# Layer 1's mixer: sixteen weight tiles split one stage ahead, the solve's copies and merges spread among products, the convolution's branch within the scan

## The chip, the cores and the metric

The kernel runs on one core of a Trainium2 chip. The metric is device time in microseconds (us) from one launch, on inputs that lie in HBM. Five engines work side by side on their own instruction queues: PE (TensorE, matmuls; PEld are its weight loads), DVE (VectorE), ACT (ScalarE), POOL (GpSimd) and SP (SyncE, which here issues nearly all DMA transfers). Each takes its instructions strictly in the order written at build time, and waits at one until what it needs is there.

## The reference

A backbone of two layers over 512 tokens: 256 context tokens and 256 latent tokens, 1024 channels, in fp32. Context tokens read only context; the latent scans start from the context's final state.

```python
for l in range(2):
    h += 0.5 * gate1 * swiglu(mod(rmsnorm(h)), ffn1)          # "ffn1"
    n = mod(rmsnorm(h)); p = n @ w_in                         # "mixer"
    a = conformer_conv(p[conv])          # GLU, 31 taps per row of 64, LayerNorm, silu, @ conv_proj
    q, k, v = silu(short_conv(p[qkv]))   # 3 taps; q, k normalised
    o = gated_delta_rule(q, k, v, ...)   # 8 heads, two directions, in chunks: a triangular solve, then a scan
    b = (rmsnorm(o) * onorm * silu(p[z])) @ dn_proj
    h += gate2 * ((sigmoid(p[ga]) * a + sigmoid(p[gb]) * b) @ w_out)
    h += 0.5 * gate3 * swiglu(mod(rmsnorm(h)), ffn2)          # "ffn2"
out = rmsnorm(h_latent)
```

## The kernel before

**Products.** Activations lie with channels on the 128 partitions and tokens in columns. An fp32 product is made of three passes on tiles rounded to a short format: high by high, high by low, low by high. So every weight tile of 128 x 8 x 128 values (512 KB) passes three steps in `weights`: SP loads it into `raw` (L124; the pool `rawp` has 3 buffers), ACT writes its rounded half `whi` (L117), DVE writes the rest `wlo` as `raw` minus `whi` (L118; the pool `wp` has 3 buffers for each half). Then PE makes 24 matmuls from it into a bank of PSUM named `pm` (L147). The bank is emptied by ACT or DVE, and there are 4 of them. Other uses of PSUM share 4 banks named `px`. In layer 1 the gates, the convolution and q need only the latent tokens (256 columns, in the rows `128x256`); k and v need all 512.

**Background.** `beside` hands a stage a list of jobs, and every call of `weights` draws from it at an even rate. In ffn1 of layer 0 there are 57 jobs for 64 calls (the modulation's `ada` weights: a load of 512 KB and four DVE instructions each); in ffn1 of layer 1 there are 24 for 64.

**The mixer**, in the order of its code:

- the convolution's input (GLU), k and q, with their norms;
- `todo`, a list of 32 products: 8 gate tiles each of z, ga and gb (`gate`: ACT empties the bank into `gz` at L964 and stores it to DRAM), then 8 value tiles (`value`: a short convolution on ACT and DVE, L450 and L451, then transposes by PE, L976). `some(n)` writes out the next n of them;
- `gram` and `solve`: the triangular blocks of 32 x 32 are inverted on DVE by 31 steps of an outer product, behind 16 copies `G` of diagonal blocks by ACT (L604), and ended by the transposes `XT` (L626) and `XB` (L638);
- `merge_blocks`: blocks of 32 are merged to 64 and to 128, in 12 groups of small matmuls (L664; L674 and L677; L701; L712). Between a group and the instructions that read its bank stands a point where a product may be written. `MERGE[l] = (before, every)` says how many products of `todo` come ahead of the first group, and that every so many-th point takes one of the rest;
- `conv`: 8 channel tiles of 31 taps (`cy`, L834 and L836, on DVE) with sums in `ysum`; the tiles go to DRAM as `y`. A call for priority (`CP`) lets layer 0's taps move ahead among the products; the framework's scheduler sets each engine's queue at build time, and in layer 1 too the taps stand as filling among the splits;
- `scan`: 16 steps of four heads. A step needs `bv` (L737), a product with the state (`residue`, L766, L769), the solved values (L775), and in the second half, for the latent tokens, the outputs (L789 with `qt`, L790 with `pt`). `pt`, `qt` and `q` come back from DRAM by loads on SP (L751, L755, L757); `q` has one buffer, `qt` and `pt` two;
- `PLAN[l]` gives 14 indices: at which step of the scan the six pieces of `conv_norm` (the LayerNorm of the convolution, which loads `y` back as `yc`, L857) and the eight products of `conv_proj` (`branch`) are written. Indices from 16 on are behind the scan, where each is followed by one product of `dn_proj`;
- `out_norm` (the norm of the scan's output, POOL at L895, transposes at L903), the products of `dn_proj`, then `w_out` in `residual`.

`branch(..., last)` multiplies a product by its gate (`g`, loaded back from DRAM). The one that comes first stores to DRAM as `m` (L1037); the last one loads that as `other`, adds it (L1034) and splits the sum for `w_out`.

Of the kernel before, what the change touches and what calls it, by code (L numbers as in the profile page):

```python
# [12 lines left out]
F32 = mybir.dt.float32  # L13
F32R = mybir.dt.float32r
# [13 lines left out]

PLAN = ((0, 2, 3, 4, 4, 5, 6, 7, 9, 11, 15, 15, 16, 16), (13, 14, 15, 16, 17, 18, 24, 24, 24, 24, 24, 24, 24, 24))
MERGE = ((19, 1), (28, 2))
CP = (1000, 0)


# [4 lines left out]
def blk(b):  # L40
    return slice(32 * b, 32 * b + 32)
# [9 lines left out]
class Net:  # L51
# [3 lines left out]
    def __init__(self, ctx, tc, a, out):  # L55
        self.tc, self.nc, self.a, self.out = tc, tc.nc, a, out
        nc = tc.nc
        pool = lambda name, bufs, **kw: ctx.enter_context(tc.tile_pool(name=name, bufs=bufs, **kw))
        self.cp = pool("cp", 1)
        self.vp = pool("vp", 2)  # L60
        self.sp = pool("sp", 2)
        self.rawp = pool("rawp", 3)
        self.wp = pool("wp", 3)
        self.hp = pool("hp", 1)
        self.wk = pool("wk", 2)
        self.pm = pool("pm", 4, space=PSUM)
        self.px = pool("px", 4, space=PSUM)
        self.dp = pool("dp", 1, space=DRAM)
        self.beside([], 1)
        self.small = nc.sync  # L70
        self.homes = iter(HOMES)
        cst = lambda name, n=128: self.cp.tile([128, n], F32, name=name)
        self.ident = cst("ident")
        make_identity(nc, self.ident)
        self.ones = cst("ones")
        nc.vector.memset(self.ones, 1.0)
        self.mhalf = cst("mhalf", 16)
        nc.vector.memset(self.mhalf, -0.5)
        self.tri = [cst("tri0"), cst("tri1")]
        make_upper_triangular(nc, self.tri[0])  # L80
        make_lower_triangular(nc, self.tri[1])
        self.cap = [cst("cap0"), cst("cap1")]
        for d in range(2):
            nc.vector.tensor_scalar(out=self.cap[d], in0=self.tri[d], scalar1=-1.0, scalar2=1e6, op0=ALU.add, op1=ALU.mult)
        self.sel = cst("sel", 63)
        nc.vector.memset(self.sel, 0.0)
        nc.vector.memset(self.sel[:, 31:32], 1.0)
# [22 lines left out]
    def beside(self, jobs, calls):  # L110

        self.bg, self.rate, self.credit = jobs, len(jobs) / calls, 0.0
# [4 lines left out]
        nc.scalar.activation(out=hi, in_=x, func=AF.Copy)  # L117
        nc.vector.tensor_tensor(out=lo, in0=x, in1=hi.bitcast(F32), op=ALU.subtract)  # L118

    def weights(self, src, nk, pool=None):  # L120

        nc = self.nc
        raw = self.rawp.tile([128, 8, 128], F32, tag="raw", name="raw")
        nc.sync.dma_start(out=raw[:, :nk, :], in_=src.rearrange("(k p) m -> p k m", p=128))  # L124
        kw = dict(bufs=4) if pool else {}
        hi, lo = ((pool or self.wp).tile([128, 8, 128], F32R, tag=t, name=t, **kw) for t in ("whi", "wlo"))
        with self.tc.high_priority():
            self.split(hi[:, :nk, :], lo[:, :nk, :], raw[:, :nk, :])
        self.background()
        return hi, lo  # L130

    def column(self, src, col):

        nk, k0, out = src.shape[0] // 128, 0, []
        for g in ([8] if nk == 8 else [8, 7, 7]):
            out.append((self.weights(src[k0 * 128:(k0 + g) * 128, col:col + 128], g), k0, g))
            k0 += g
        return out
# [7 lines left out]
                for p, (u, v) in enumerate(((wh, x[0]), (wh, x[1]), (wl, x[0]))):  # L146
                    nc.tensor.matmul(ps, lhsT=u[:, j, :], rhs=v[:, k, tok], start=k == 0 and p == 0, stop=k == n - 1 and p == 2)  # L147

    def project(self, src, col, x, tok):
        ps = self.psm()  # L150
        w = self.column(src, col)
        self.mm3(ps[:, tok], w, x, tok)
        return ps

# [434 lines left out]
            if need_q:  # L589
                nc.sync.dma_start(out=psp[t], in_=pt.rearrange("p d h i -> p (d h i)"))  # L590

    def solve(self, y, R, pool):


        nc = self.nc
        dv = nc.vector
        m8 = lambda name: pool.tile([128, 2, 32, 32], F32, tag="m8", name=name)
        nbu = self.sp.tile([128, 2, 32], F32, tag="nbu", name="nbu", bufs=1)
        dv.transpose(out=nbu.rearrange("p d i -> p (d i)"), in_=y.nb.rearrange("p d t h -> p (d t h)"))
        G = m8("G")  # L600
        for s in range(2):
            for b in range(4):
                for d in range(2):
                    nc.scalar.activation(out=G[blk(b), d, s * 16:(s + 1) * 16, :],  # L604
                                         in_=R[s][blk(b), d, :, :, blk(b)].rearrange("p t h i -> p (t h) i"), func=AF.Copy)
        M = m8("M")
        dv.transpose(out=M[:, 0], in_=G[:, 0].rearrange("p u i -> p i u"))
        dv.transpose(out=M[:, 1].rearrange("p a b -> p b a"), in_=G[:, 1].rearrange("p u i -> p i u"))
        dv.tensor_tensor(out=M[:, 0], in0=M[:, 0], in1=nbu[:, 0].unsqueeze(2).to_broadcast([128, 32, 32]), op=ALU.mult)
        dv.tensor_tensor(out=M[:, 1], in0=M[:, 1], in1=nbu[:, 1].unsqueeze(1).to_broadcast([128, 32, 32]), op=ALU.mult)  # L610
        X = m8("X")
        nc.gpsimd.memset(X, 0.0)
        dv.memset(X.rearrange("p d a b -> p d (a b)")[:, :, 0:1024:33], 1.0)
        for k in range(31):
            r, c = 31 - k, k + 1
            tmp = [pool.tile([128, 256], F32, tag=f"tmp{d}", name="tmp", bufs=1)[:, :r * c].rearrange("p (r c) -> p r c", r=r)
                   for d in range(2)]
            for d in range(2):
                dv.tensor_tensor(out=tmp[d], in0=M[:, d, k + 1:, k:k + 1].to_broadcast([128, r, c]),
                                 in1=X[:, d, k:k + 1, 0:c].to_broadcast([128, r, c]), op=ALU.mult)  # L620
            for d in range(2):
                dv.tensor_tensor(out=X[:, d, k + 1:, 0:c], in0=X[:, d, k + 1:, 0:c], in1=tmp[d], op=ALU.add)

        XT = m8("XT")
        for d in range(2):
            dv.transpose(out=XT[:, d].rearrange("p u i -> p i u"), in_=X[:, d] if d == 0 else X[:, d].rearrange("p a b -> p b a"))  # L626
        return X, XT
# [279 lines left out]
    def mixer(self, y, nxt):  # L907
        nc, a, l = self.nc, self.a, y.l
        w_in = a["w_in"][l]
        streams = (0, 1) if l == 0 else (1,)  # L910
        tok = FULL if l == 0 else STREAM[1]
# [4 lines left out]
        zsp, asp, bsp, glu, ysp, msp = ([dram(f"{nm}{k}", T) for k in range(8)] for nm in ("z", "ga", "gb", "glu", "y", "m"))  # L916
        x, xctx = self.n, self.np_ctx
# [3 lines left out]
        R = [kp.tile([128, 2, 2, 8, 128], F32, name=f"R{s}") for s in range(2)]  # L921
        K = [kp.tile([128, 8, 256], F32, name=f"K{s}") for s in range(2)]
        m8 = opn("m8", self.left, 2)
# [35 lines left out]
            wait.append((r, sq4, sqs))  # L959

        def gate(dst, col, fn, sc, k):
            ps = self.project(w_in, col + k * 128, x, tok)
            t_ = self.w512("gz")
            nc.scalar.activation(out=t_[:, tok], in_=ps[:, tok], func=fn, scale=sc)  # L964
            nc.scalar.dma_start(out=dst[k][:, tok], in_=t_[:, tok])

        def value(h):
            ps = self.project(w_in, 4096 + h * 128, x, FULL)
            late.append((h, self.short_conv(y, ps, 16 + h, FULL, None)))
            if len(late) > 2:  # L970
                v_tokens(*late.pop(0))
# [10 lines left out]
        V, late = [], []  # L982
# [4 lines left out]
        def some(n):  # L987
            for _ in range(min(n, len(todo))):
                todo.pop(0)()
# [4 lines left out]
            nc.sync.dma_start(out=qsp[s], in_=Q[s].rearrange("p h t -> p (h t)"))  # L994
        self.gram(y, R, K, Q, m8, psp)
        stacks["q"].close()
        X, XT = self.solve(y, R, m8)
        before, every = MERGE[l]
        some(before - 2)
        points = iter(range(12))  # L1000
        self.merge_blocks(y, R, X, XT, m8, opn("xn", self.left), lambda: some(next(points) % every == 0))
        some(len(todo))
# [25 lines left out]
        def branch(m, gate, w, parts, last):  # L1028

            g, other = load(gate[m], "g"), load(msp[m], "other") if last else None  # L1030
            ps = self.project(w[l], m * 128, parts, tok)
            nc.vector.scalar_tensor_tensor(out=g, in0=g, scalar=1.0, in1=ps[:, tok], op0=ALU.add, op1=ALU.mult)
            if last:
                nc.vector.tensor_tensor(out=g, in0=g, in1=other, op=ALU.add)  # L1034
                self.split(mh[:, m, tok], ml[:, m, tok], g)
            else:
                nc.sync.dma_start(out=msp[m][:, tok], in_=g)  # L1037
        norm = self.conv_norm(y, ysp, ysum, tok, ytile, yh, yl)
        step = lambda: next(norm)
        conv = [lambda m=m: branch(m, asp, a["conv_proj"], (yh, yl), l == 1) for m in range(KT)]  # L1040
        dn = [lambda m=m: branch(m, bsp, a["dn_proj"], (oh, ol), l == 0) for m in range(KT)]
        beside = {}
        for i, f in zip(PLAN[l], [step] * 6 + conv):
            beside.setdefault(i, []).append(f)
# [45 lines left out]
def build(ctx, tc, a, out):  # L1090
# [37 lines left out]
    net.mixer(y[0], (y[0], 2))  # L1128
    y[1] = net.layer(1)
    net.ffn(y[0], 2, (0, 1), (y[1], 0), vectors(y[1], net.ada(y[1], range(6))))  # L1130
    net.ffn(y[1], 0, (0, 1), (y[1], 1), net.ada(y[1], range(6, 9)))
    net.mixer(y[1], (y[1], 2))
    net.ffn(y[1], 2, (1,), None, [])
    net.finish()
# [18 lines left out]
```

## Time and profile before

| what | value |
|---|---|
| time, median of 3 runs | 2468.5 us (2466.74 to 2470.38) |
| the profiled execution: its own time | 2473.86 us |
| span of its instructions | 2471.9 us |
| PE busy | 2378.4 us, 96% of the span |
| DVE busy | 1774.5 us, 72% |
| ACT busy | 976.3 us, 39% |
| granted clock of PE, mean | 0.986 |

The profile is of one execution, so its rows are set against its own 2473.86 us. A busy PE is one with a matmul in its pipe; the granted clock is a share of full speed. In the trace, ffn1 of layer 1 runs from about 1418 to 1805 us, the mixer of layer 1 from there to about 2272 us (the inverse's products and gates to about 2045, the merge to about 2105, the scan to about 2176), and the last ffn2 to the end.

### The profile page before, as it was taken

The page shows a single profiled execution, that of the slowest core. Times are in us where ns is not written, and L with a number is a line of the kernel's source. Part 1 is how long each engine was busy: PE and PEld are TensorE (multiplying, and loading weights), DVE is VectorE, ACT ScalarE, POOL GpSimd, SP SyncE. Part 2 cuts the span into 40 slices and gives each one's busy share as a digit, 9 for nine tenths or more (in the row PEclk, how much of TensorE's full clock was granted, in tenths as well). Part 3 has the DMA queues.
Part 4 walks back from the last instruction along what each step waited for, and adds up shares of the span by engine and source line. Part 5 has one row for each costly group of instructions (what it writes and reads, how often), then busy time and mean ns, then how long its engine had stood idle before and what let it go on. Part 6 is the DMA issues. An engine that isn't in the chain of part 4 may idle for free. (4 is left out here: it accounts for less than half of the span.)

```text
span 2471.9 us, 38425 instructions
## 1 busy us (share of the span) xinstructions
PE 2378.4 (96%) x15099; PEld 2043.2 (83%) x15099; DVE 1774.5 (72%) x3025; ACT 976.3 (39%) x1690; POOL 41.1 (2%) x103
## 2 busy tenths in 40 slices
PE   7999999999999999999999999999989998978998
PEld 5878878887887887888788888888888897978998
DVE  4767777899999766576766575554479998966554
ACT  3222223635444733332322232222257646544443
POOL 0000000000000000000000000000000000000000
PEclk9999999999999999999999999999999998999999
DMA  8556665644653465355555444444366672355664
GB/s 257 170 165 179 177 177 174 194 125 133 196 149 113 143 216 164 116 159 163 163 161 170 138 129 136 123 134 133 113 219 162 183 200 69 105 186 169 196 184 140
DMA packets 565622, 394.62 MB, mean 160 GB/s; under 512 B 27576, under 2 KB 513090, under 8 KB 562754
## 3 DMA queue, kind: packets, MB, share of 16 engines
q1 hardware_dynamic: 555606, 371.33, 51.3%
q10 hardware_dynamic: 8684, 12.45, 1.5%
q0 software_dynamic: 1152, 8.39, 0.8%
q8 instruction: 118, 1.93, 0.3%
q14 instruction: 62, 0.51, 0.1%
HBM read 358.43 MB, written 33.69 MB: 159 GB/s over the span
## 5 line engine op out<-in xcount | busy, mean ns | idle before, releaser
L147 PE MATMUL pm<-nh,whi 128*128 128x512 f32 (+1 forms) x2544 | 899.8, 355 | 10.7 <-ACT gz L964 5.4
L147 PE MATMUL pm<-nh,wlo 128*128 128x512 f32 (+1 forms) x2544 | 896.0, 353 | 3.5 <-DVE wlo L118 3.4
L147 PE MATMUL pm<-nl,whi 128*128 128x512 f32 (+1 forms) x2544 | 896.0, 353 | 0.0
L117 ACT ACTIVATE whi<-raw 128x1024 fp32r<-128x1024 f32 (+1 forms) x450 | 469.3, 1044 | 1067.6 <-PE pm L147 833.1
L118 DVE TENSOR_TENSOR wlo<-raw,whi 128x1024 fp32r<-128x1024 f32 (+1 forms) x450 | 540.6, 1203 | 208.5 <-ACT whi L117 206.0
L147 PEld LDWEIGHTS pm<-nh,whi 128*128 128x128 f32 x2544 | 482.1, 190 | 92.3 <-ACT whi L117 12.5
L147 PEld LDWEIGHTS pm<-nh,wlo 128*128 128x128 f32 x2544 | 482.0, 190 | 69.3 <-DVE wlo L118 4.7
L147 PEld LDWEIGHTS pm<-nl,whi 128*128 128x128 f32 x2544 | 482.4, 190 | 64.4 <-DVE nl L381 0.6
L301 DVE SCALAR_TENSOR_TENSOR aacc<-adaw,sc,aacc 128x512 f32<-128x512 f32 x448 | 312.0, 746 | 152.8 <-DMA adaw<-ada_w_in 152.7
L836 DVE SCALAR_TENSOR_TENSOR cy<-cx,cdw,cy 128x512 f32<-128x512 f32 (+1 forms) x480 | 273.3, 610 | 1.8
L147 PE MATMUL pm<-gh,whi 128*128 128x512 f32 (+1 forms) x770 | 268.2, 348 | 1.7 <-DVE h L386 1.7
L147 PE MATMUL pm<-gl,whi 128*128 128x512 f32 (+1 forms) x770 | 266.7, 346 | 0.0
L147 PE MATMUL pm<-gh,wlo 128*128 128x512 f32 (+1 forms) x770 | 266.5, 346 | 0.0
L147 PEld LDWEIGHTS pm<-gh,whi 128*128 128x128 f32 x770 | 145.0, 188 | 26.3 <-ACT whi L117 3.4
L147 PEld LDWEIGHTS pm<-gh,wlo 128*128 128x128 f32 x770 | 145.1, 188 | 18.7 <-issue 0.8
L147 PEld LDWEIGHTS pm<-gl,whi 128*128 128x128 f32 x770 | 145.1, 188 | 17.6
L436 DVE TENSOR_TENSOR silu<-silu,pm 128x512 f32<-128x512 f32 (+1 forms) x88 | 54.4, 618 | 70.5 <-PE pm L147 65.2
L386 DVE SCALAR_TENSOR_TENSOR h<-pm,gate,h 128x256 f32<-128x256 f32 x80 | 36.4, 480 | 63.0 <-PE pm L147 62.8
L117 ACT ACTIVATE gh<-silu 128x512 fp32r<-128x512 f32 (+1 forms) x88 | 50.5, 574 | 37.7 <-DVE silu L436 37.5
L380 ACT ACTIVATE nh<-t,mods 128x256 fp32r<-128x256 f32 x88 | 39.8, 501 | 60.2 <-DVE t L377 60.2
L118 DVE TENSOR_TENSOR gl<-silu,gh 128x512 fp32r<-128x512 f32 (+1 forms) x88 | 54.4, 618 | 0.0
L147 PE MATMUL pm<-mh,whi 128*128 128x256 f32 (+1 forms) x152 | 47.6, 315 | 2.3 <-ACT mh L117 2.3
(249 smaller groups left out, 2383.9 us busy)
## 6 DMA issues: line engine op xcount, KB each, us to landing
raw<-ffn_w_in SPq DMA_DIRECT2D x208, 512.0 KB, 4.0
adaw<-ada_w_in SPq DMA_DIRECT2D x144, 512.0 KB, 3.8
raw<-w_in_in SPq DMA_DIRECT2D x130, 512.0 KB, 4.2
raw<-ffn_w_in SPq DMA_DIRECT2D x64, 448.0 KB, 3.9
R<-grow POOLq DMA_DIRECT2D x8, 1024.0 KB, 11.0
raw<-conv_proj_in SPq DMA_DIRECT2D x16, 512.0 KB, 6.5
raw<-dn_proj_in SPq DMA_DIRECT2D x16, 512.0 KB
raw<-w_out_in SPq DMA_DIRECT2D x16, 512.0 KB, 4.1
```

What stands on the lines that cost most here:

```text
L117: nc.scalar.activation(out=hi, in_=x, func=AF.Copy)
L118: nc.vector.tensor_tensor(out=lo, in0=x, in1=hi.bitcast(F32), op=ALU.subtract)
L147: nc.tensor.matmul(ps, lhsT=u[:, j, :], rhs=v[:, k, tok], start=k == 0 and p == 0, stop=k == n - 1 and p == 2)
L301: nc.vector.scalar_tensor_tensor(out=st.acc[:, s], in0=wt[:, j], scalar=c, in1=st.acc[:, s], op0=ALU.mult, op1=ALU.add)
L380: nc.scalar.activation(out=nh[:, k, st], in_=t1, func=AF.Identity, bias=B)
L386: self.nc.vector.scalar_tensor_tensor(out=self.h[:, m, st], in0=ps[:, st], scalar=y.gate[:, q, m, s:s + 1], in1=self.h[:, m, st], op0=ALU. ...
L436: nc.vector.tensor_tensor(out=t, in0=t, in1=pb[:, tok], op=ALU.mult)
L836: nc.vector.scalar_tensor_tensor(out=dst, in0=src, scalar=w, in1=dst, op0=ALU.mult, op1=ALU.add)
```

## The change

Three parts, all but one of them in layer 1.

1. `halve`: ffn1 of layer 1 gets 32 more background jobs beside its 24. Sixteen times, one job loads a weight tile of `w_in` and splits it, and the next stores both halves to DRAM. The tiles are every other one of z, ga, gb and of the values. In the mixer `weights` then loads the two halves of such a tile (two transfers of 512 KB in rows of 4 KB) straight into `whi` and `wlo`, with no split.
2. `solve` writes one product of `todo` after every second block of `G` copies (4 in all; both layers). The count ahead of the merge falls by 4, and in layer 1 `MERGE` becomes (24, 1): 24 products ahead, and a value product at each of the first 8 points.
3. `PLAN` of layer 1: `conv_norm` at steps 6 to 11 (13 to 18 before), the products of `conv_proj` at 12 to 18 (all at 24 before, behind the scan). In layer 1 too the convolution's branch now comes first and stores `m`; that of `dn_proj` is the last.

```diff
-PLAN = (..., (13, 14, 15, 16, 17, 18, 24, 24, 24, 24, 24, 24, 24, 24))
-MERGE = ((19, 1), (28, 2))
+PLAN = (..., (6, 7, 8, 9, 10, 11, 12, 13, 14, 15, 15, 16, 17, 18))
+MERGE = ((19, 1), (24, 1))
...
     def weights(self, src, nk, pool=None, parts=None):
         nc = self.nc
+        if parts:
+            out = tuple(self.wp.tile([128, 8, 128], F32R, tag=t, name=t) for t in ("whi", "wlo"))
+            for t, part in zip(out, parts):
+                nc.sync.dma_start(out=t.rearrange("p k m -> p (k m)").bitcast(F32), in_=part)
+            self.background()
+            return out
...
+    def halve(self, src, key):
+        nc = self.nc
+        self.parts[key] = parts = [self.dp.tile([128, 1024], F32, name=f"{n}_{key[0]}_{key[1]}") for n in ("hi", "lo")]
+        def job():
+            raw = self.rawp.tile([128, 8, 128], F32, tag="raw", name="raw")
+            nc.sync.dma_start(out=raw, in_=src.rearrange("(k p) m -> p k m", p=128))
+            hi, lo = (self.wp.tile([128, 8, 128], F32R, tag=t, name=t) for t in ("whi", "wlo"))
+            self.split(hi, lo, raw)
+            late.extend(zip(parts, (hi, lo)))
+        def store():
+            for d, t in late:
+                nc.sync.dma_start(out=d, in_=t.rearrange("p k m -> p (k m)").bitcast(F32))
+        late = []
+        return [job, store]
...
         for s in range(2):
             for b in range(4):
                 for d in range(2):
                     nc.scalar.activation(out=G[...], in_=R[s][...], func=AF.Copy)
+                if b % 2:
+                    beside()
...
-        X, XT = self.solve(y, R, m8)
+        X, XT = self.solve(y, R, m8, lambda: some(1))
         before, every = MERGE[l]
-        some(before - 2)
+        some(before - 6)
...
-        conv = [lambda m=m: branch(m, asp, a["conv_proj"], (yh, yl), l == 1) for m in range(KT)]
-        dn = [lambda m=m: branch(m, bsp, a["dn_proj"], (oh, ol), l == 0) for m in range(KT)]
+        conv = [lambda m=m: branch(m, asp, a["conv_proj"], (yh, yl), False) for m in range(KT)]
+        dn = [lambda m=m: branch(m, bsp, a["dn_proj"], (oh, ol), True) for m in range(KT)]
...
-    net.ffn(y[1], 0, (0, 1), (y[1], 1), net.ada(y[1], range(6, 9)))
+    jobs, w_in = net.ada(y[1], range(6, 9)), a["w_in"][1]
+    halves = [net.halve(w_in[:, c:c + 128], (1, c)) for c0 in (5120, 6176, 7200, 4096) for c in range(c0, c0 + 1024, 256)]
+    net.ffn(y[1], 0, (0, 1), (y[1], 1), [f for i in range(24) for f in jobs[i:i + 1] + sum(halves[i:i + 1], [])])
```

**Place 1: the end of the inverse, on DVE.** Before, DVE's queue holds these rows at the end of layer 1's `solve` (`cy` are taps of the convolution, `sconv` the short convolution of a value or of q and k):

```order
L450 SCALAR_TENSOR_TENSOR sconv<-pm,dns,sconv 128x2x255
L622 TENSOR_TENSOR X<-X,tmp 128x31
L626 STREAM_TRANSPOSE XT<-X 128x32x32 x2
L451 SCALAR_TENSOR_TENSOR sconv<-pm,dns,sconv 128x2x255
L638 STREAM_TRANSPOSE XB<-X 128x32x32
L118 TENSOR_TENSOR wlo<-raw,whi 128x1024
L450 SCALAR_TENSOR_TENSOR sconv<-pm,dns,sconv 128x2x255
L638 STREAM_TRANSPOSE XB<-X 128x32x32
L451 SCALAR_TENSOR_TENSOR sconv<-pm,dns,sconv 128x2x255
L841 TENSOR_TENSOR ysum<-ysum,cy 128x256
L836 SCALAR_TENSOR_TENSOR cy<-cx,cdw,cy 128x256
```

The changed kernel has there (its L655 is L626 of before, L667 is L638, L863 and L865 are the taps, L696 reads the first merge group):

```order
L651 TENSOR_TENSOR X<-X,tmp 128x31
L655 STREAM_TRANSPOSE XT<-X 128x32x32 x2
L667 STREAM_TRANSPOSE XB<-X 128x32x32 x2
L865 SCALAR_TENSOR_TENSOR cy<-cx,cdw,cy 128x256
L863 TENSOR_SCALAR cy<-cx,cdw,v_9346 128x256
L865 SCALAR_TENSOR_TENSOR cy<-cx,cdw,cy 128x256 x4
L696 TENSOR_TENSOR Y<-px,bm 128x16x32
L865 SCALAR_TENSOR_TENSOR cy<-cx,cdw,cy 128x256 x5
L119 TENSOR_TENSOR wlo<-raw,whi 128x1024
```

Both transposes `XB` now follow `XT` at once. From the `MEMSET` of `X`, at the inverse's start, to the last `XB`, 18 splits stand in DVE's queue before and 7 after. Counted from the mixer's start to the scan's first `bv`, it has 65 splits before and 49 after, and 203 taps before and 235 after.

**Place 2: the loads of gates and values, on SP.** Before, the queue runs as follows from the store of the last `psp` on (the 20 loads are gates and values in a row):

```order
L124 DMA raw<-w_in_in 128x8x128
L590 DMA psp_1_14866<-pt 128x2048
L124 DMA raw<-w_in_in 128x8x128 x20
L837 DMA y_1_14904<-cy 128x256
L828 DMA cx<-glu_1_14898 128x4x64
L124 DMA raw<-w_in_in 128x8x128 x2
L124 DMA raw<-dn_proj_in 128x8x128 x4
```

The changed kernel alternates there between a whole tile and the two halves of one (numbers in the names are columns of `w_in`):

```order
L131 DMA raw<-w_in_in 128x8x128
L127 DMA whi<-hi_7200_12230 128x1024
L127 DMA wlo<-lo_7200_12231 128x1024
L127 DMA whi<-hi_7456_12232 128x1024
L127 DMA wlo<-lo_7456_12233 128x1024
L131 DMA raw<-w_in_in 128x8x128 x2
L127 DMA whi<-hi_7712_12234 128x1024
L127 DMA wlo<-lo_7712_12235 128x1024
L131 DMA raw<-w_in_in 128x8x128
L127 DMA whi<-hi_7968_12236 128x1024
L127 DMA wlo<-lo_7968_12237 128x1024
L131 DMA raw<-w_in_in 128x8x128
```

Each `whi` and `wlo` is a load into a buffer of `wp`, so it waits on SP until PE has done with the tile that lay in that buffer, three tiles ago; the whole tile behind it in the queue waits as well.

**Place 3: the end of the scan, on PE and SP.** Before, PE's queue near the scan's end holds nothing but the scan and the convolution's mean (L848):

```order
L789 MATMUL px<-S_18653,qt 128x128
L790 MATMUL px<-bv,pt 128x128
L848 MATMUL px<-ysum,ones 128x256
L775 MATMUL pm<-bv,R_14921 128x128 x4
L789 MATMUL px<-S_18652,qt 128x128
L790 MATMUL px<-bv,pt 128x128
```

In the changed kernel products of `conv_proj` (`yh`, `yl`) stand among the scan's matmuls (L795 is L766 of before, L804 is L775, L818 and L819 are L789 and L790):

```order
L174 MATMUL pm<-yh,whi 128x256
L174 MATMUL pm<-yl,whi 128x256
L174 MATMUL pm<-yh,wlo 128x256
L795 MATMUL pm<-S_18781,K_15083 128x128
L804 MATMUL pm<-bv,R_15081 128x128 x4
L174 MATMUL pm<-yh,whi 128x256
L818 MATMUL px<-S_18781,qt 128x128
L819 MATMUL px<-bv,pt 128x128
```

Of the 192 matmuls of `conv_proj`, 86 now stand ahead of the scan's last group of outputs, 34 between it and the first transposes of `out_norm`, and 72 behind those; before, all 192 stood behind. On SP the last loads of the scan stood among those of `yc` before:

```order
L857 DMA yc<-y_1_14905 128x256
L757 DMA q<-q_1_14868 128x4x128
L857 DMA yc<-y_1_14906 128x256
L857 DMA yc<-y_1_14907 128x256
L751 DMA pt<-psp_1_14865 128x512
L755 DMA qt<-grow_15213 128x512
L857 DMA yc<-y_1_14908 128x256
L757 DMA q<-q_1_14868 128x4x128
L1049 DMA h<-hsp_14862 128x4096
```

Now the load of `h` (2 MB) and those of the gate `ga` stand ahead of the last two loads of `q`, and the stores of `m` ahead of the very last:

```order
L780 DMA pt<-psp_1_15026 128x512
L1078 DMA h<-hsp_15022 128x4096
L1052 DMA g<-ga_1_15037 128x256
L786 DMA q<-q_1_15028 128x4x128
L1052 DMA g<-ga_1_15038 128x256
L780 DMA pt<-psp_1_15025 128x512
L784 DMA qt<-grow_15373 128x512
L1066 DMA m_1_15069<-g 128x256
L1052 DMA g<-ga_1_15039 128x256
L1052 DMA g<-ga_1_15040 128x256
L1066 DMA m_1_15070<-g 128x256
L786 DMA q<-q_1_15028 128x4x128
```

In layer 0 the order of PE's instructions in the mixer is the same before and after.

## Rows read from the trace of the kernel before

**Rows 1.** The page, busy time: engine, us, share of the span, instructions.
```profile
PE 2378.4 (96%) x15099; PEld 2043.2 (83%) x15099; DVE 1774.5 (72%) x3025; ACT 976.3 (39%) x1690; POOL 41.1 (2%) x103
```

**Rows 2.** Windows: stretch, us, busy of each engine, PE's clock, DMA share, GB/s.
```profile
60.00:400.00 340.00, 338.85 (x1533) 274.30 (x1532) 251.31 (x374) 94.59 (x125) 0.00 (x0) 1.00 0.60 177
1418.00:1805.00 387.00, 384.11 (x1897) 322.72 (x1897) 205.66 (x304) 114.76 (x160) 3.61 (x8) 1.00 0.44 128
1805.00:1850.00 45.00, 37.49 (x309) 36.43 (x309) 28.59 (x55) 22.46 (x42) 2.20 (x5) 0.98 0.72 241
1850.00:1950.00 100.00, 99.94 (x635) 86.70 (x636) 98.27 (x185) 69.97 (x152) 0.69 (x6) 0.97 0.58 160
1950.00:1980.00 30.00, 25.05 (x218) 24.77 (x216) 27.93 (x50) 19.09 (x29) 3.07 (x8) 0.96 0.70 211
1980.00:2045.00 65.00, 64.59 (x461) 61.24 (x462) 65.00 (x155) 27.78 (x43) 2.05 (x3) 0.96 0.71 191
2045.00:2105.00 60.00, 51.85 (x1045) 43.14 (x1043) 52.56 (x103) 39.59 (x61) 0.45 (x4) 0.86 0.27 76
2105.00:2145.00 40.00, 38.53 (x339) 37.74 (x337) 38.20 (x106) 25.51 (x71) 0.00 (x0) 1.00 0.23 71
2145.00:2181.00 36.00, 24.03 (x164) 22.25 (x165) 26.30 (x72) 11.25 (x47) 1.67 (x1) 0.88 0.60 191
...
2209.00:2244.00 35.00, 30.93 (x252) 29.55 (x251) 20.67 (x36) 13.08 (x17) 0.00 (x0) 1.00 0.85 246
```

**Rows 3.** Windows, from the scan's end to the mixer's end.
```profile
2176.00:2272.00 96.00, 79.97 (x608) 76.05 (x608) 63.72 (x118) 42.45 (x82) 4.70 (x4) 0.94 0.63 182
```

**Rows 4.** PE's waits, 1975 to 2105 us: for whom, total us, times, longest.
```profile
PE pm L147 <- ACT gz L964: 5.4, 1, 5.4
PE px L677 <- issue: 4.2, 2, 2.2
PE px L674 <- issue: 3.0, 1, 3.0
```

**Rows 5.** PE's waits in the scan, 2105 to 2176 us.
```profile
PE px L789 <- DVE qt L758: 5.7, 3, 2.8
PE px L789 <- issue: 1.1, 2, 0.6
```

**Rows 6.** PE's waits, 2176 to 2272 us.
```profile
PE px L903 <- DVE o L897: 5.0, 2, 4.8
PE px L338 <- DVE acc L330: 2.7, 1, 2.7
PE pm L147 <- ACT mh L117: 2.3, 2, 1.7
```

**Rows 7.** The chain that ended last, 2053 to 2095 us: start, us, what.
```profile
2053.57 5.79 PE pm L147 x24
...
2068.59 8.03 PE pm L147 x24
...
2082.94 7.71 PE pm L147 x24
```

**Rows 8.** DVE's groups by form, 1850 to 2272 us: count, busy us, mean ns, idle.
```profile
L836 DVE SCALAR_TENSOR_TENSOR cy<-cx,cdw,cy 128x256 f32<-128x256 f32 x232 | 100.6, 477 | 0.4
L118 DVE TENSOR_TENSOR wlo<-raw,whi 128x1024 fp32r<-128x1024 f32 x81 | 98.9, 1224 | 18.3 <-ACT whi L117 18.1
```

**Rows 9.** SP's timeline, 1940 to 2060 us: start, us, issues.
```profile
1968.92 63.77 SPq L124 DMA_DIRECT2D raw<-w_in_in  x20
```

**Rows 10.** DMA issues of the whole span: count, size, median us to landing.
```profile
raw<-w_in_in SPq DMA_DIRECT2D x130, 512.0 KB, 4.2
...
psp<-pt SPq DMA_DIRECT2D x6, 1024.0 KB, 4.2
```

**Rows 11.** The chain that ended last, 2132 to 2272 us.
```profile
2157.13 4.17 DMA q<-q
2161.33 0.70 DVE qt L758
2162.05 4.50 DMA q<-q
```

More of the change, by code (lines that the diff above doesn't have):

```diff
@@ L24 @@
 STREAM = (slice(0, 256), slice(256, 512))
-PLAN = ((0, 2, 3, 4, 4, 5, 6, 7, 9, 11, 15, 15, 16, 16), (13, 14, 15, 16, 17, 18, 24, 24, 24, 24, 24, 24, 24, 24))
-MERGE = ((19, 1), (28, 2))
+PLAN = ((0, 2, 3, 4, 4, 5, 6, 7, 9, 11, 15, 15, 16, 16), (6, 7, 8, 9, 10, 11, 12, 13, 14, 15, 15, 16, 17, 18))
+MERGE = ((19, 1), (24, 1))
 CP = (1000, 0)
@@ L69, in __init__ @@
         self.beside([], 1)
+        self.parts = {}
         self.small = nc.sync
@@ L118, in split, with weights @@
         nc.vector.tensor_tensor(out=lo, in0=x, in1=hi.bitcast(F32), op=ALU.subtract)
-    def weights(self, src, nk, pool=None):
+    def weights(self, src, nk, pool=None, parts=None):
         nc = self.nc
+        if parts:
[4 more added lines that the diff above has]
+            return out
         raw = self.rawp.tile([128, 8, 128], F32, tag="raw", name="raw")
@@ L130, in weights, with column @@
         return hi, lo
-    def column(self, src, col):
+    def halve(self, src, key):
[12 more added lines that the diff above has]
+        return [job, store]
+    def column(self, src, col, parts=None):
         nk, k0, out = src.shape[0] // 128, 0, []
+        if parts:
+            return [(self.weights(None, 8, parts=parts), 0, 8)]
         for g in ([8] if nk == 8 else [8, 7, 7]):
@@ L147, in mm3, with project @@
                     nc.tensor.matmul(ps, lhsT=u[:, j, :], rhs=v[:, k, tok], start=k == 0 and p == 0, stop=k == n - 1 and p == 2)
-    def project(self, src, col, x, tok):
+    def project(self, src, col, x, tok, parts=None):
         ps = self.psm()
-        w = self.column(src, col)
+        w = self.column(src, col, parts)
         self.mm3(ps[:, tok], w, x, tok)
@@ L590, in gram, with solve @@
                 nc.sync.dma_start(out=psp[t], in_=pt.rearrange("p d h i -> p (d h i)"))
-    def solve(self, y, R, pool):
+    def solve(self, y, R, pool, beside):
         nc = self.nc
@@ L961, in gate @@
         def gate(dst, col, fn, sc, k):
-            ps = self.project(w_in, col + k * 128, x, tok)
+            ps = self.project(w_in, col + k * 128, x, tok, self.parts.get((l, col + k * 128)))
             t_ = self.w512("gz")
@@ L967, in value @@
         def value(h):
-            ps = self.project(w_in, 4096 + h * 128, x, FULL)
+            ps = self.project(w_in, 4096 + h * 128, x, FULL, self.parts.get((l, 4096 + h * 128)))
             late.append((h, self.short_conv(y, ps, 16 + h, FULL, None)))
```

## The prediction

> **What bounds the kernel now.** I read the page's busy times first: PE is busy 2378 of 2472 us [rows 1]. The change takes no matmul away and adds none, so it can only win back PE's idle time, and time in which PE runs at a lower clock. Next came the windows, stage by stage, to see where such time lies [rows 2]. Ffn1 of layer 1 is dense (384.1 of 387 us). In the mixer of layer 1 PE is full from 1850 to 1950 and from 1980 to 2045, and DVE is as full there (98.3 of 100, and 65.0 of 65). PE loses 5 us from 1950 to 1980, 8 in the merge (2045 to 2105), 1.5 and 12 in the scan's two windows, and 16 between the scan and the mixer's end [rows 2, 3]. Then the waits, to put names to these holes. PE waits 5.4 us for the bank that ACT empties at L964, and 7.2 us in the merge's small matmuls [rows 4]. In the scan it waits 5.7 us for `qt` [rows 5]; behind the scan 5.0 us for the normed `o`, and some smaller waits [rows 6]. Last, the chain: a value product in the merge takes 8.03 and 7.71 us where the one just before the holes took 5.79 [rows 7], in a window whose granted clock is 0.86, that is with part of it at 1.2 instead of 2.4 GHz, behind short idle stretches. So holes cost twice.
>
> Up to the scan, DVE is the engine to count. From 1850 to 2105 us it is busy 98.3 + 27.9 + 65.0 + 52.6 = 243.8 of 255 us [rows 2], and the inverse's chain (31 dependent steps), the splits and the taps share its queue. The scan's first `bv` can't start before that work is through. PE, with 241.4 busy us in the same windows, is about level with it.
>
> **Part 1, the halves; the term up to the scan.** Sixteen splits leave DVE's work in the mixer, each 98.9/81 = 1.22 us [rows 8]: 19.6 us. What fills the room is told at place 1 of the change: 32 taps more stand ahead of the first `bv`, each 100.6/232 = 0.43 us [rows 8]: 13.9 us. Net 5.7 us less DVE work ahead of the scan: I take **-6**. PE must shrink with it, and can: it has 13 idle us in those four windows, the 5.4 us wait for `gz` is filled by the four products among the `G` copies, and the merge's 7.2 us [rows 4] by value products of about 5.8 us at every one of its first eight points. Bounds: 0 if the order binds otherwise, -13 if DVE's 7.4 idle us from 2045 to 2105 [rows 2] go too.
>
> The halves' loads cost transfers. A pair of gates makes 24 matmuls twice at 30.93/252 = 0.123 us each (a window of 256-column products at full clock [rows 2]), or 5.9 us. Before, it moves two raw tiles and two 128 KB stores, 1.31 MB. SP's row agrees roughly: 20 loads in 63.8 us, 3.2 us each [rows 9]. After, it moves one raw tile, two halves and two stores: 0.52 + 1.05 + 0.26 = 1.83 MB. How fast can that go? From 1980 to 2045 us 191 GB/s took 0.71 of the DMA engines, so 269 GB/s would fill them; by 1805 to 1850, 241 at 0.72, it is 335 [rows 2]. At 269 the pair takes 6.8 us, 0.9 us too long, times 12 pairs +11. At 335 it takes 5.5 us: 0. Halves are whole rows of 4 KB, unlike a raw tile's runs of 512 bytes, and a 1 MB store in long rows lands in the 4.2 us that a raw tile of half the size takes [rows 10]. So the upper speed is nearer: **+3**, bounds 0 and +11.
>
> The Trainium skill ("DMA: Bandwidth & Descriptors", section "Where 436 GB/s comes from") puts a core's share of HBM at about 358 GB/s. An estimate by that page is 5.1 us for the pair, and the term would be 0. The rows here have no stretch above 246 GB/s, so they neither reach that limit nor deny it.
>
> In ffn1 of layer 1 sixteen splits and 25 MB in and out are added to a stage that moves 128 GB/s at a DMA share of 0.44 and has DVE busy 206 of 387 us. It would then move about 193 GB/s with DVE at 0.58. In ffn1 of layer 0, 57 jobs run beside 64 calls at 177 GB/s, a share of 0.60 and DVE at 0.74, and PE is busy 338.9 of 340 us [rows 2]. So **0**. If the cover fails (a half's buffers stay taken until its stores have landed), I bound it at 1 us of PE for each: +16. Layer 0's mixer keeps its PE order: 0, give or take 2.
>
> **Part 2 and 3 in the scan.** Of the 192 `conv_proj` matmuls 86 move ahead of the last output group: 86 x 0.123 = 10.6 us of PE work in a stage whose two windows have 13.5 idle us, 6.8 of them before the outputs [rows 2, 5], plus 2.9 us lost to the clock (24.03 busy at 0.88). DVE's load there is not worse: 32 taps (13.9 us) leave it, while `conv_norm`'s arithmetic and some seven splits (8.6 us) enter. Not all of it fits: the products stand at fixed places in PE's queue, and while PE runs 20 of them the next step of the scan, if ready, waits. Moreover each `q` load takes 4.2 to 4.5 us, one at a time since `q` has one buffer [rows 11]; they are a chain of their own. I take **+3**; bounds 0 (all hidden) and +10 (nothing hidden).
>
> **Behind the scan.** Those 86 matmuls are gone: -10.6. The 34 that stand between the last output group and the first transposes (34 x 0.123 = 4.2 us) fill most of the 5.0 us wait for `o` [rows 6]: -4.2. The stretch's 608 matmuls would take 608 x 0.123 = 74.6 us at full clock and take 79.97 [rows 3]; of these 5.4 us I give back 1. In sum **-16**; bounds -10 (only the move) and -21 (half of the 16 idle and 5.4 slow us as well). The waits for the residual's sums and for `mh` (2.7 and 2.3 us [rows 6]) stay; `mh` now comes from the branch of `dn_proj`.
>
> **Sum.** -6 + 3 + 0 + 3 - 16 = -16. The profiled execution took 2473.9 us, so the changed one would take 2457.9; it lies 5.4 above the median, and on the median's scale that is 2452.5.
>
> **The rivals.**
>
> *Halves come late (slower).* The halves' loads wait on SP until PE releases a buffer, three tiles back, so a pair of halves has the two products in between, 5.9 us, to land, and the raw tile behind it in the queue waits along. If the halves go no faster than raw tiles do (4.2 us each [rows 10], one behind the other), a pair takes 8.4 us, 2.5 us too long: 12 x 2.5 = 30 in place of +3, and the -6 is worth nothing to a PE that waits for weights. Then 0 + 30 + 3 - 16 = +17: 2485. It decides from 5.9 + (16 + 3)/12, about 7.5 us for a pair with the -6 kept; 0.4 us more puts it beyond what can be told from no change. For it: the stage already uses 0.71 of the DMA engines [rows 2]. Against: both halves can be in flight together, and the 1 MB store in 4.2 us [rows 10].
>
> *The halves are paid for in ffn1 (no change).* The +16 above eats the gain: 2468. For it: every half takes a slot of a pool of three that PE needs. Against: ffn1 of layer 0, where as many jobs cost nothing, though those hold no slot of `wp`.
>
> *The scan's loads become its chain (smaller gain).* `h`, 2 MB, now stands ahead of the last two `q` loads; at the 4.2 us that 1 MB takes [rows 10] it holds the DMA engines 8.4 us, and the last `q` stands behind stores of `m` that wait for products. That is +8 on the scan: 2460. For it: PE already waits for `qt` three times [rows 5].
>
> *A larger gain.* All DVE holes go before the scan (-13), transfers are hidden (0), the scan absorbs its products (0) and the tail closes up (-21): -34, 2434.
>
> **How the numbers follow.** The forecast with its own range, 2440 to 2459, gets 0.48; the larger gain 0.10; the scan's chain 0.12; payment in ffn1 0.12; late halves 0.18. About 0.2% (5 us) is what a measurement here can tell from no change. The first three end below 2463.5: faster 0.70. The fourth is the same: 0.12. Late halves are slower: 0.18. The single bounds add up to -34 (2434, the larger gain itself) and to 0 + 11 + 16 + 10 - 10 = +27 (2495). The range 2434 to 2474 takes in all of the first four cases and leaves out most of the late halves (0.15).
>
> **What would show it.** In the changed profile: no wait above 2 us for `gz` around the solve; merge groups with value products between them, with clock near 1.0 and value products at 5.8 us; the scan's first `bv` about 3 us earlier, counted from the mixer's start; 86 `yh` matmuls within the scan and the wait for `o` below 1 us; ffn1 of layer 1 still 387 us. PE waits for DMA at `whi` or `wlo` between 1950 and 2100 us would show the late halves; more than 6 us for `qt` in the scan would show the scan's chain. The prediction is wrong if the order on DVE was not what held the scan back, or if the loads of the gates are what binds next.

## The result and the profile after

The changed kernel takes 2451.32 us (median of 4 runs, 2448.28 to 2452.73); before, 2469.44 us beside it. The ratio is 0.992, 95% interval 0.9905 to 0.9936: 0.8% faster. The forecast was 2452.5. The profiled execution has a span of 2451.0 us against 2471.9 before: 20.9 us less.

The page of the changed kernel, busy times, answers to [rows 1]:

```profile
span 2451.0 us, 38568 instructions
...
PE 2371.5 (97%) x15099; PEld 2035.0 (83%) x15099; DVE 1776.3 (72%) x3025; ACT 977.9 (40%) x1690; POOL 41.0 (2%) x103
```

PE is busy 7 us less, at a mean granted clock of 0.992 against 0.986; the other 14 us of the gain were idle time. Windows of the changed kernel (columns as in [rows 2]); the cuts lie at the end of ffn1, around the inverse, at the last `XB` (2038), at the first `bv` (2101), at the first output matmul (2131.5), and behind the scan:

```profile
1418.00:1805.00 387.00, 384.88 (x1879) 320.87 (x1879) 222.01 (x314) 131.29 (x175) 2.51 (x7) 1.00 0.63 191
...
1950.00:1980.00 30.00, 28.61 (x248) 28.41 (x248) 27.42 (x56) 17.38 (x28) 3.31 (x10) 1.00 0.76 258
1980.00:2038.00 58.00, 51.27 (x388) 48.16 (x386) 52.99 (x145) 17.28 (x30) 1.81 (x1) 0.97 0.89 287
2038.00:2101.00 63.00, 60.27 (x1097) 49.35 (x1098) 61.28 (x126) 38.70 (x59) 0.46 (x4) 1.00 0.31 98
2101.00:2131.50 30.50, 29.73 (x258) 28.86 (x259) 27.45 (x75) 22.29 (x63) 0.00 (x0) 1.00 0.37 109
2131.50:2179.00 47.50, 43.93 (x380) 43.17 (x380) 36.77 (x96) 25.35 (x79) 2.73 (x2) 1.00 0.66 199
2179.00:2251.00 72.00, 61.52 (x479) 59.44 (x478) 48.59 (x85) 29.28 (x46) 2.33 (x2) 0.94 0.69 203
```

Four things are to be seen. The stall of 5 us at the `G` copies is gone (28.6 of 30). The gates are now the stage with holes: 6.7 us of PE's 58, at a DMA share of 0.89. From the last `XB` to the scan PE and DVE are both nearly full (60.3 and 61.3 of 63 us), at full clock, where the clock was 0.86 [rows 2]. And the scan's second half, 12 us idle before, is 3.6 us idle, with conv products in it. PE's waits in the gate stage (1950 to 2040 us) name the new hole:

```profile
PE pm L174 <- DMA wlo<-lo: 5.5, 6, 1.8
PE px L693 <- issue: 1.5, 1, 1.5
PE pm L174 <- DMA whi<-hi: 1.4, 3, 0.9
```

And the chain of the changed kernel from there on shows why, and what the merge has become (start, us, what):

```profile
1998.46 7.50 DMA wlo<-lo
...
2012.25 7.52 DMA wlo<-lo
...
2053.05 5.79 PE pm L174 x24
...
2061.63 5.78 PE pm L174 x24
```

The two halves on the chain land 7.5 us after their issue (the `whi` halves from 1950 to 2040 us take 5.6 us in the median), and two gates take 5.9 us. Value products in the merge take 5.8 us instead of 8.03 and 7.71 [rows 7].

To compare all runs I cut each trace at the same five events: the first product of layer 1's ffn1, the mixer's first product, the scan's first `bv`, its last output matmul (L790 of before), and the first product of the last ffn2. Chips and executions shift whole traces by some us. In us, from one profiled execution of each kernel, with PE's wait for the sum of the taps (at L848 of before) beside:

| kernel | ffn1 | to first `bv` | scan | to ffn2 | sum | wait at L848 |
|---|---|---|---|---|---|---|
| before | 370.7 | 306.9 | 70.3 | 97.0 | 844.8 | none |
| changed | 373.6 | 301.6 | 73.4 | 78.0 | 826.6 | none |
| plan alone | 370.7 | 303.5 | 90.3 | 76.1 | 840.6 | 14.6 |
| plan undone | 374.5 | 301.3 | 70.6 | 94.2 | 840.6 | none |
| halves undone | 370.7 | 305.8 | 94.3 | 75.4 | 846.1 | 18.0 |
| halves alone | 374.2 | 303.9 | 70.4 | 96.3 | 844.8 | none |
| part 2 undone | 374.7 | 304.0 | 72.9 | 77.2 | 828.7 | none |
| plan alone, 27 taps | 370.6 | 306.1 | 74.5 | 77.7 | 828.9 | none |
| before, 27 taps | 370.7 | 302.3 | 70.6 | 95.4 | 838.9 | none |
| 8 values, 8 gates | 374.8 | 304.0 | 73.6 | 75.8 | 828.3 | none |
| 20 halves | 374.0 | 299.6 | 72.6 | 74.5 | 820.6 | none |
| 24, 16 of them gates | 382.9 | 302.9 | 75.2 | 76.6 | 837.6 | none |
| 24, 8 of them keys | 381.5 | 302.5 | 74.7 | 76.2 | 835.0 | none |
| 32 halves | 403.0 | 305.8 | 72.0 | 77.9 | 858.7 | none |

How far can a single execution be trusted? From the mixer's first product to the first `bv`, before and plan alone run the same instructions, on DVE in the same order, and so do the two runs with 27 taps. Yet that stage takes 306.9 and 303.5 us in the one pair, 302.3 (before) and 306.1 (plan alone) in the other. In the 64 us ahead of the first `bv` the granted clock is 0.87 and 0.92 in the first pair, 0.95 and 0.87 in the second: the longer one has the lower clock. So differences of up to 4 us in that column say nothing of an edit. The sums, too, differ from the measured ratios by 5 us (before with 27 taps) and 7 us (8 keys), in the other runs by 2 or less.

### The profile page after: what moved, and what is told of

It reads as the page before. It is cut to its first block, busy times and chain, and to the rows that moved or that the text cites. A ratio compares the mean times of both kernels' runs of the same rounds, so it can differ in the third digit from the quotient of the medians.

```text
span 2451.0 us, 38568 instructions
## 1 busy us (share of the span) xinstructions
PE 2371.5 (97%) x15099; PEld 2035.0 (83%) x15099; DVE 1776.3 (72%) x3025; ACT 977.9 (40%) x1690; POOL 41.0 (2%) x103
## 4 chain that ended last, share of the span: by engine, by line
PE 59%; issue 18%; DVE 14%; DMA 7%; ACT 1%; POOL 1%; SPq 0%; DVEq 0%; POOLq 0%; ACTq 0%
PE pm L174 51%; DVE cy L865 4%; DVE wlo L119 3%; DMA adaw<-ada_w_in 1%; DMA raw<-w_in_in 1%; DMA raw<-ffn_w_in 1%; PE px L812 1%; DMA wlo<-lo 1%; DVE tmp L648 1%; PE pm L804 1%; DVE X L651 1%; PE pm L795 1%; PE px L819 1%; DVE aacc L328 1%; ACT whi L118 1%
## 5 line engine op out<-in xcount | busy, mean ns | idle before, releaser
L865 DVE SCALAR_TENSOR_TENSOR cy<-cx,cdw,cy 128x512 f32<-128x512 f32 (+1 forms) x480 | 271.8, 608 | 2.1
L174 PE MATMUL pm<-ml,whi 128*128 128x256 f32 (+1 forms) x152 | 48.6, 320 | 2.2 <-DVE ml L119 2.2
```

What stands on the lines that cost most here:

```text
L865: nc.vector.scalar_tensor_tensor(out=dst, in0=src, scalar=w, in1=dst, op0=ALU.mult, op1=ALU.add)
```

## The experiments

The theory at the start (A): the parts need each other, since only the halves make room on DVE for the taps ahead of the scan. The rival (B): the parts add up, as the sum of the prediction has it, and the plan alone carries the gain behind the scan.

**Plan alone.** On the kernel before, only:

```diff
-PLAN = (..., (13, 14, 15, 16, 17, 18, 24, 24, 24, 24, 24, 24, 24, 24))
+PLAN = (..., (6, 7, 8, 9, 10, 11, 12, 13, 14, 15, 15, 16, 17, 18))
-        conv = [... branch(m, asp, a["conv_proj"], (yh, yl), l == 1) ...]
-        dn = [... branch(m, bsp, a["dn_proj"], (oh, ol), l == 0) ...]
+        conv = [... branch(m, asp, a["conv_proj"], (yh, yl), False) ...]
+        dn = [... branch(m, bsp, a["dn_proj"], (oh, ol), True) ...]
```

> Only the third part: conv_norm at steps 6 to 11 and conv_proj at 12 to 18, dn_proj last; no halves, copies and merges as before. Theory A (the parts need each other: only the halves make room on DVE for the taps ahead of the scan): 208 taps stand ahead of the scan's first bv as before, so some 14 us of taps still lie in the scan, now ahead of the mean; the products wait for them and the scan grows by 8 to 12 us, the time falls by 8 us at most (2461). Theory B (the parts add up, the third alone carries the gain behind the scan): scan +3, behind it -20, so -17 (2452).

Measured: ratio 0.9987 (0.9971 to 1.0002), no change that can be told. The stretch behind the scan is 20.9 us shorter, and the scan 20.0 us longer, twice what A expected. As before, 203 taps stand ahead of the first `bv` (not 208). PE's timeline of this run shows where:

```profile
2146.57 1.22 PE L848 MATMUL px<-ysum,ones 128*128 128x256 f32 x2 [14.56 <-DVE ysum L841]
```

The matmul for the mean of the convolution stands in PE's queue in the middle of the scan. It waits 14.6 us for the last taps, and the scan's own matmuls stand behind it. After the wait a group of eight of them takes 1.91 us where it took 1.06 before it; the granted clock from 2105 to 2152 us is 0.82. DVE's timeline just ahead of it has the taps:

```profile
2135.10 10.95 DVE L836 SCALAR_TENSOR_TENSOR cy<-cx,cdw,cy 128x256 f32<-128x256 f32 x21
2146.09 0.42 DVE L841 TENSOR_TENSOR ysum<-ysum,cy 128x256 f32<-128x256 f32 x1
```

In the changed kernel the same matmul has no wait. The sum is done on DVE (first line) 6.6 us before PE comes to it (second line):

```profile
2117.84 0.41 DVE L870 TENSOR_TENSOR ysum<-ysum,cy 128x256 f32<-128x256 f32 x1
2124.88 0.60 PE L877 MATMUL px<-ysum,ones 128*128 128x256 f32 x2
```

B falls here: the plan by itself is worth nothing.

**Plan undone.** The changed kernel with those lines as before.

> The changed kernel with the third part undone: the plan of before, conv_proj behind the scan and last. Both theories: the scan's first bv about 4 us earlier as in the changed kernel, nothing gained behind it: 2465. Theory A allows a few us more in the scan, since 32 taps have left it: 2461. If the scan is held by its loads of q, no difference there.

Measured: 0.9983 (0.9973 to 0.9993), 0.2% faster. The scan starts 5.6 us earlier, counted from the mixer's first product, but ffn1 pays 3.8. The 32 taps that left the scan are worth nothing there (70.6 us against 70.3): without the new plan PE has no wait for them.

**Halves undone.** The changed kernel with ffn1's jobs as before:

```diff
-    net.ffn(y[1], 0, (0, 1), (y[1], 1), [f for i in range(24) for f in jobs[i:i + 1] + sum(halves[i:i + 1], [])])
+    net.ffn(y[1], 0, (0, 1), (y[1], 1), net.ada(y[1], range(6, 9)))
```

> The changed kernel without the halves: the 16 tiles are loaded and split in the mixer as before, copies, merges and plan as changed. Theory A: 16 splits (19.6 us) are back on DVE, XB comes 8 us later and the taps run into the scan, so the gain is 8 to 10 us smaller than with halves: 2460. Theory B (the halves lose on transfers what they save on DVE: PE waits 6.9 us for them in the changed kernel): as fast as the changed kernel or up to 3 us faster, 2448 to 2452; no PE wait for a DMA at whi or wlo, and 387 us in ffn1.

Measured: 1.0001 (0.9989 to 1.0013). The whole gain is gone: A was too mild, and B, by which the halves cost as much as they save, is out. In DVE's queue 41 taps fewer stand ahead of the first `bv` than in the changed kernel, and the wait for their sum is the longest of all, 18.0 us:

```profile
2156.69 1.22 PE L877 MATMUL px<-ysum,ones 128*128 128x256 f32 x2 [18.02 <-DVE ysum L870]
```

**Halves alone.** The kernel before with `halve` and its loads, but copies, merges and plan as before.

> The kernel before with the halves alone: solve, merge order and plan as before. Theory A: DVE's work ahead of the scan falls by 6 us and the scan starts 3 us earlier: 2465. Theory B: the transfers cost the 7 us that PE waits for them in the changed kernel, and without products among copies and merges nothing is won back: 2472 to 2476.

Measured: 1.0007 (0.9993 to 1.002). The scan starts 3.0 us earlier, as A has it, but that is within what the column shows without an edit; ffn1 takes 3.5 us more. The time follows neither account.

**Plan alone with 27 taps.** The direct test of A, on the plan alone; it leaves out part of the convolution:

```diff
-            for j in range(31):
+            for j in range(27 if y.l == 1 else 31):
```

> The plan alone, with the last four of the 31 taps left out in layer 1 (32 DVE instructions fewer, about 14 us; the convolution is then another one). Theory A (the taps that lie in the scan are what the third part pays for): the wait of PE for the sum of the taps at L848, 14.6 us in the plan alone, falls below 3 us, the gain behind the scan is kept, and the time falls by 14 to 20 us against the kernel before. Rival (the products within the scan lengthen it by themselves, and the wait only takes the place of another): the scan stays some 15 us longer, and no more than 4 us are gained.

Measured: 0.9929 (0.9902 to 0.9956). The wait is gone and the scan is 74.5 us instead of 90.3:

```profile
2133.83 0.60 PE L848 MATMUL px<-ysum,ones 128*128 128x256 f32 x2
```

**Before with 27 taps**, as control: the same edit on the kernel before.

> The kernel before with the last four of the 31 taps left out in layer 1 (the convolution is then another one): what fewer taps are worth without the new plan. Theory A (taps cost only where the plan makes PE wait for their sum): 0 to 3 us faster than before. Rival (DVE's work bounds the mixer as such): 10 to 14 us faster, and then the gain of the plan with 27 taps says nothing of the plan.

Measured: 0.9995 (0.9977 to 1.0013). Taps by themselves cost nothing that can be told, while the plan on top of 27 taps is worth 0.9929/0.9995, about 0.7% (each ratio is against the kernel before on its own chip). Theory A stands: what the halves are for is to get the last taps off DVE before PE comes to their sum.

**Part 2 undone.** The changed kernel with `before - 2`, (28, 2) and no products among the copies.

> The changed kernel with the second part undone: halves and plan as changed, copies and merges as before. If the merges' interleave only moves waits about ahead of a DVE that sets the scan's start anyway: 0 to 4 us slower than the changed kernel (2452 to 2455 on the scale of before at 2468.5). If the interleave is what wins the merge's holes back (L677 ends 19 us earlier in the changed kernel), 8 to 12 us slower.

Measured: 0.9935 (0.9913 to 0.9958), against 0.992 for the changed kernel on other chips. The first merge matmuls (L664 of before) come 15 us later, yet the scan starts only 2.4 us later and the sum of stages is 2.1 us longer, both too little to be told from none. The first reading fits: the interleave closes holes in PE ahead of a DVE that has as much to do. Where the taps are late it may do harm: from the plan alone to the run without halves, which adds the interleave, the stages grow by 5.5 us; by the times (0.9987 and 1.0001, intervals that overlap) this isn't shown.

**Values and 8 gates.** Sixteen halves, other tiles:

```diff
-    halves = [... for c0 in (5120, 6176, 7200, 4096) for c in range(c0, c0 + 1024, 256)]
+    gates, values = [c0 + k * 128 for c0 in (5120, 6176, 7200) for k in range(8)], [4096 + k * 128 for k in range(8)]
+    halves = [net.halve(w_in[:, c:c + 128], (1, c)) for c in gates[::3] + values]
```

> Sixteen halves as in the changed kernel, but all 8 value tiles and every third gate. If PE's waits of 6.9 us for halves among the gates come from the DMA engines being full there (share 0.89), the traffic of the gate stage falls by a tenth and the waits fall to 2 to 4 us; the time is 2 to 4 us below the changed kernel. If they come from the order on SP (a half waits for PE to release a buffer), the waits go by the count of halves: 8 instead of 12, 4.6 us, and the time is the same within 2 us.

Measured: 0.9932 (0.9905 to 0.9959), the same as the changed kernel. PE's waits among the gates (1960 to 2048 us):

```profile
PE pm L174 <- DMA wlo<-lo: 5.0, 6, 1.5
PE pm L174 <- ACT gz L993: 3.5, 2, 1.8
PE pm L174 <- DMA whi<-hi: 1.8, 2, 1.3
```

With 8 tiles in halves among the gates instead of 12 the waits for them are 6.8 us again, not 2 to 4 and not 4.6: neither account holds.

**Twenty halves**: `gates[::2] + values`.

> Twenty halves: all 8 value tiles and every second gate. Theory A (DVE's work ahead of the scan decides): 4 splits fewer, all taps ahead of the scan, scan start 0 to 5 us earlier than in the changed kernel: 0 to 5 us faster. If transfers and PE hold the gates and values by now (PE 60.3 of 63 us from XB to the first bv), the same within 2 us.

Measured: 0.9906 (0.9876 to 0.9937), in the profile the shortest span of all, 2447.7 us. The last tap starts 1.7 us behind the first `bv` (15 us in the changed kernel), and every stage of the mixer is a little shorter. The sum of stages is 6.0 us less, but the intervals of the two ratios overlap: that it beats the changed kernel isn't shown.

**Twenty-four halves, 16 gates**: `gates[::3] + gates[1::3] + values`.

> Twenty-four halves: 16 of the 24 gates and all 8 values. With twenty the mixer took 446.7 us from its first product to ffn2's first (452.9 in the changed kernel, 474.0 before), with DMA shares of 0.91 among the gates. If DVE's work is still what binds, another 2 to 4 us come off the mixer. If the transfers of the gates bind (16 pairs of halves in 24 gates: 0.7 + 0.17 + 0.13 MB for one gate, about 1.0 MB in 2.95 us, 340 GB/s where 305 were moved), the mixer is 2 to 6 us longer than with twenty; in both cases ffn1 pays 1 us more.

**Twenty-four halves, 8 keys**: the key tiles and `gates[::3] + values`, and `parts` handed to the product of k.

> Twenty-four halves again, but 8 of them key tiles (products of 5.8 us, ahead of the gates), 8 values and every third gate. If the gates' transfers bind and splits taken out anywhere ahead of the scan free DVE: as many splits fewer as in the run with 16 gates, but waits for halves of 3 to 5 us in place of more; the mixer is the shortest of all, 440 to 446 us, and the time 26 to 30 us below before. If DVE's work before the inverse counts for nothing (the inverse's start is set by other work), the mixer stays at 450 to 454 us.

Measured: 0.9979 (0.9967 to 0.9992) and 0.9987 (0.9978 to 0.9996). Both lose most of the gain, and not where I expected: ffn1 takes 382.9 and 381.5 us, 9 and 8 more than with twenty. The mixer is 3 us longer than with 20 halves up to the first `bv` and 2 to 3 us in the scan, so no expectation of a shorter one came true, though fewer splits are left and all taps lie ahead of the scan. The other readings fared better. With 16 gates the mixer is 8 us longer than with twenty halves (2 to 6 were expected if the transfers bind), and PE's waits for halves among the gates rise from 7.0 to 10.9 us. With 8 keys it takes 453.4 us (450 to 454 if DVE's work before the inverse counts for nothing). Neither cause is isolated. PE's waits in ffn1 of the run with 16 gates (1428 to 1800 us):

```profile
PE px L274 <- ACT adas L271: 5.9, 3, 4.3
```

**All 32 as halves** (`range(32)` for the jobs).

> All 24 gates and 8 values as halves: no split is left in that stage. The rival of late halves, driven to its end: a gate moves 1.05 + 0.13 = 1.18 MB; at the 287 GB/s seen among the gates in the changed kernel that is 4.1 us instead of 2.95, so PE loses 24 x 1.15 = 28 us there; the mixer is 15 to 30 us longer than in the changed kernel and most of the gain is lost. If the engines can move 400 GB/s, it loses nothing (2.95 us).

Measured: 1.0053 (1.003 to 1.0076), slower than before. That is paid in ffn1, 403.0 us, 32 more than before. The mixer is only 3 us longer than in the changed kernel, not 15 to 30. The gates hold, with the DMA engines busy nearly all the time. A window of that run among its gates:

```profile
2015.00:2054.00 39.00, 35.01 (x285) 33.91 (x285) 39.00 (x135) 4.67 (x13) 1.81 (x1) 1.00 0.98 355
```

The transfer rate that I had taken as the limit, 287 GB/s, was not one: 355 GB/s were moved at a share of 0.98. PE waits 7.5 us for halves from 1985 us to the scan, hardly more than with twelve tiles in halves.

## Why the prediction was right

The forecast was -16 us; the profiles say -20.9, the medians -18.1. Of the profiles' difference -18.2 lies in the four stages of the table, -1.5 ahead of them and -1.2 in the last ffn2, which the forecast left alone. Of the signs that the prediction named, two failed: the wait for `o` is 1.6 us, not below 1, and ffn1 grew; and PE's waits for `whi` and `wlo`, the sign of the late halves, are there.

**Up to the scan** the forecast was -3 (-6 for DVE, +3 for transfers). From the mixer's first product to the first `bv` it is -5.3 against before and -1.9 against plan alone, which has the same instructions there. So the sign is likely right, and the size isn't shown. Nor are the two terms singly: PE waits 6.9 us for halves, but how much of that delays the scan isn't known, since DVE is busy 53 of the same 58 us. What the copies and merges do is seen in PE: the wait of 5.4 us for `gz` [rows 4] is gone, and the merge runs at a clock of 1.00. The late halves, my rival on the slow side, are real as a wait (up to 7.5 us from issue to landing where 5.9 us are to be had), but not at its price of 30.

**Ffn1** was put at 0 and costs 2.9 us (373.6 against 370.7), and 3.5 to 4.1 in the other runs with sixteen halves. PE's waits there stay under 1 us each in the changed kernel. The trace shows another cause: the 24 small matmuls that sum the modulation's columns (L306 of before). Before, they stand in PE's queue as three groups of eight, and a group is done in 1.07 us (first line). In the changed kernel one group is split by products into two, four and two, and a piece of two takes as long as the eight did; another group, whole, takes 1.87 us:

```profile
1661.01 1.07 PE L306 MATMUL px<-aacc,ones 128*32 128x512 f32 x8
1700.02 1.04 PE L333 MATMUL px<-aacc,ones 128*32 128x512 f32 x2
1763.97 1.87 PE L333 MATMUL px<-aacc,ones 128*32 128x512 f32 x8
```

From the start of one to the start of the next instruction, all 24 take 3.0 us before and 5.7 in the changed kernel, 2.7 of the 2.9 us. In the other runs with sixteen halves they take 3.3 to 4.0 us more than before, and these stages are 3.5 to 4.1 us longer; without halves both are as before. The argument by cover looked at busy shares, not at these matmuls and their place in PE's queue; why a whole group takes longer isn't shown. With 20 halves (64 jobs for 64 calls) ffn1 costs 3.3 us, 2.4 of them here. Beyond that other costs come in: 24 halves (72 jobs) cost 11 to 12 us though the 24 matmuls take 3.0 to 3.2 again, and 32 (88 jobs) cost 32.

**The scan** was put at +3: it is +3.1. The products fill the holes, and PE waits 2.9 us for `qt` instead of 5.7 [rows 5]:

```profile
PE px L818 <- DVE qt L787: 2.9, 2, 1.7
```

The rival of the scan's loads did not come; `h` ahead of the last two loads of `q` costs nothing that shows.

**Behind the scan** was put at -16: -19.0. Windows from the last output matmul to ffn2, before and then the changed kernel:

```profile
2175.80:2272.30 96.50, 79.99 (x609) 76.05 (x608) 64.16 (x119) 42.75 (x83) 4.70 (x4) 0.94 0.63 181
2174.90:2252.60 77.70, 66.14 (x515) 63.76 (x513) 51.99 (x91) 33.05 (x63) 2.33 (x2) 0.93 0.69 203
```

PE's idle time there falls from 16.5 to 11.6 us, by 4.9 where I had 4.2. The wait for `o` gives 3.4 of it: the first transposes wait 1.6 us instead of 5.0 [rows 6]. PE's busy time falls by 13.9 us. The 86 matmuls that moved are 10.6 of it, as counted; the other 3.3, for which I had 1, are eight small matmuls of `conv_norm` that moved too, and products that take less time. The granted clock of the whole stretch didn't rise (0.94 and 0.93).

**What the sum did not say** is that its terms hang together. It books the 32 taps ahead of the scan as a cost of 13.9 us in the first term and the gain behind the scan as free of conditions. The runs show the reverse: without the taps ahead, the third part gains nothing that can be told (0.9987), and without the third part, the first two gain 0.2%. The wait that decides, PE's for the sum of the taps in the middle of the scan, is in none of my rivals; I had looked at `q`, at stores and at weights, but not at the matmul of the mean that the new plan moves from the scan's end to its middle. The forecast came out right because in the changed kernel this wait is avoided, by 6.6 us: the last taps lie at the scan's beginning. The prediction had not asked for that, so this part of its success is luck.

**What stays open**: why PE waits 5 to 8 us for halves with 8, 12 or 24 tiles in halves among the gates, and 10.9 with 16; what of the low clock ahead of the scan comes from the edits; what makes ffn1 so much longer from 72 jobs on; and why 24 halves make the mixer longer than 20 though DVE has less to do.

## What to carry to other kernels

When a change has several parts, ask of each which wait it would end in alone; a part that looks like an outlay in the sum (taps pulled forward) may be the condition of another's gain. When an instruction moves earlier in an in-order queue, find its latest input first, since all that stands behind it will wait for that input. Work pushed into an earlier dense stage cost 3 to 4 us here with up to one job for each call and 11 us and more beyond; look there at the order of the matmuls too, not only at busy shares.

## What the runs showed of the hardware

Transfers mostly in rows of 4 KB moved more for the same busy share of the DMA engines than a stage of tiles in runs of 512 bytes: 355 GB/s at a share of 0.98 with all tiles in halves, where the gates of the kernel before moved 191 GB/s at 0.71, that is an estimated 269 for a full share [rows 2].

The Trainium skill ("DMA: Bandwidth & Descriptors", section "Where 436 GB/s comes from") puts a core's share of HBM at about 358 GB/s. The 355 GB/s, a mean over 39 us, lie near it, but it was no ceiling here: from 2000.5 to 2012.7 us the same run moved 413 GB/s, and the kernel before 395 from 1838.75 to 1847 us, inside a window whose mean is 241 [rows 2]. So the estimate of 5.1 us for a pair was not a lower bound, and the trace of before held faster stretches than its rows showed.

Small matmuls (`128*32` in the rows) took 1.07 us for eight in a row, and 1.04 us for two by themselves; another eight took 1.87.
